# Two loads traced under another engine's squares, two casts moved to GpSimd, and three frame loads moved ahead of the small rows, at the beginning of a streaming encoder trunk

## The chip, the core and the metric

The kernel runs on one core of one Trainium2 chip. The metric is the device time of one execution in microseconds (us). Each run is timed several times; the profile is of one more execution, which has a time of its own and, inside it, a span from its first to its last instruction. The core's engines work side by side, each through its own list of instructions in order: PE (TensorE, matmul and transpose), DVE (VectorE), ACT (ScalarE), POOL (GpSimd) and SP (SyncE, which here issues most of the loads and stores). An instruction can carry waits on semaphores that other engines and transfers raise; until they are met, the engine stands and everything behind it in its list stands too.

## The reference

One layer over 2080 frames (2048 of a prompt, 32 of a running stream) of width 1024, all in float32:

```python
hn = rmsnorm(h, g_mix)
proj = hn @ w_in                       # 1024 x 3072
hA, bA, cA, zA, vB, zB = split(proj)   # six blocks of 512 columns
yA = bA * (causal width-3 conv of cA * hA + bias) * silu(zA)
yB = (windowed mean of vB - vB, mapped per group, scaled) * silu(zB)
h = h + concat([yA, yB]) @ w_out
h = h + (p @ w_ple) * sigmoid(rmsnorm(h, g_ple) @ w_gate)
y = rmsnorm(h, g_final)
```

The histories of the convolution and of the pooling are outputs as well. Only the first two lines concern the change: the norm of the first frames and their first products with `w_in`.

## The kernel before

**Arithmetic.** A float32 product is made of three products of parts: each operand is split into a rounded high part ("hi") and the rest ("lo"), and hi·hi, hi·lo and lo·hi are added up in one PSUM bank. The hi part is a cast (ACT `copy`), the lo part a subtraction (DVE `tensor_tensor`).

**Blocks.** The prompt's frames are worked on in blocks of 416 (three tiles of 128 rows and one of 32). In the first stage two blocks are in memory at once. Frames come in with rows on partitions, are squared and summed on ACT (`sumsq`), POOL makes the reciprocal root of the mean from the sum in two small instructions (`rstd_of`, lines 70 and 74), DVE scales the rows, PE transposes them into PSUM, and from there the hi and lo parts are made.

**Beginning.** For block 0 the order is written out by hand (lines 608 to 683): three tiles and the two 32-row pieces `short0` are loaded, `first_normal` scales, `first_turn` transposes, `first_hi` and `first_lo` make the parts. The raw columns of the first three weights (`zb`, `v`, `c`; 512 KB each) are loaded by `raw_weight`, and their hi parts are cast on ACT (lines 673 and 691), their lo parts subtracted on DVE (lines 682 and 695). `first_products` then runs hi·hi, weight-hi·frame-lo and weight-lo·frame-hi, each for `zb`, `v` and `c` in turn, eight matmuls at a time. Between these products the generator `second_block` is stepped: it loads the three tiles of block 1 (line 712), scales them with `normal` (line 406), transposes them, splits them into hi and lo (line 724: ACT, line 78, then DVE, line 81), copies them back to memory (line 725) and forms sums and differences (from line 734). After that come `zb`, `v` and `c` of block 1 with the usual three parts, matmul by matmul (line 572), and then the rest of the stage.

**Six small vectors** (convolution weights, biases, histories) are loaded into the tile `rows` (lines 751 to 756), turned by one transpose into `pv`, and the pooling weights are loaded into `raw_pw` (line 769).

**What sets the order.** The kernel is traced in program order and a planner then orders each engine's list by costs it assumes; the lists are fixed when the program is built. `keep_in_program_order` (in `in_turn`) ties an instruction to the one traced before it on its engine. `tc.issue_after(ins)` ties what its block traces *on the engine of* `ins` to a place behind `ins` in that engine's list; it is a matter of order in the list, not a wait. Buffers come in rings: `xin` has five tiles for frames, `raws` four for raw columns, `ps_m` six PSUM banks. A load into a ring's next tile waits until the last reader of the tile's former content is done. SP's loads also share eight semaphores in turn, so that the ninth load waits until the first has landed, and so on.

Of the kernel before, what the change touches and what calls it, by code (L numbers as in the profile page):

```python
# [28 lines left out]
KH = KC // 2  # L29
# [5 lines left out]
def trunk(ctx, tc, x_p, x_s, c_conv, c_pool, p_p, p_s, g_mix, w_in, conv_w, conv_b, pool_w,  # L35
          pool_scale, w_out, g_ple, w_gate, w_ple, g_fin, y_p, y_s, sc_p, sp_p, sc_s, sp_s):
    nc = tc.nc
# [29 lines left out]
    def rstd_of(ssq, n, name, r=None):  # L67

        ms = sm.tile([P, 1], F32, tag="ms", name=f"ms_{name}")
        nc.gpsimd.tensor_scalar(ms[:n], ssq[:n], scalar1=1.0 / D, scalar2=EPS,  # L70
                                op0=ALU.mult, op1=ALU.add)
        if r is None:
            r = sm.tile([P, 1], F32, tag="rstd", name=f"rstd_{name}")
        nc.gpsimd.tensor_tensor(r[:n], ms[:n], nhalf[:n], op=ALU.pow)  # L74
        return r
# [10 lines left out]
    g_bc = const.tile([P, D], F32, name="g_bc")  # L86
    junk = const.tile([P, D], mybir.dt.bfloat16, name="junk")

    def sumsq(x, n, name, r=None, later=False):
        ssq = sm.tile([P, 1], F32, tag="ssq", name=f"ssq_{name}")  # L90
        ins = nc.scalar.activation(junk[:n], x[:n], AF.Square, accum_out=ssq[:n])  # L91
        if later:
            tc.keep_in_program_order(ins)
        return rstd_of(ssq, n, name, r)
# [206 lines left out]
    def ring4(t, name):  # L301
        return t.tile([P, D], F32, tag="t", name=name)
# [21 lines left out]
    with ExitStack() as s1:  # L324
# [45 lines left out]
        def fill(n, t):  # L370

            for _ in range(n):
                tc.keep_in_program_order(nc.tensor.transpose(t[:, :P], ident, ident))
# [7 lines left out]
        def x_rows(tb, c):  # L381
            r = tb * NB + c * P
            if c < 3:
                return x_p[r:r + P]
            return x_p[r:r + DEC] if tb < 4 else x_s

        def x_load(name, rows):

            t, at = ring4(xin, f"xt_{name}"), 0
            for src in rows:  # L390
                m = src.shape[0]
                nc.sync.dma_start(t[at:at + m], src)
                at += m
            return t, at, f"x{name}"

        def x_stat(x, later=False):

            t, n, name = x
            return t, n, sumsq(t, n, name, later=later)

        def x_tile(name, rows):
            return x_stat(x_load(name, rows))
# [103 lines left out]
        def raw_weight(kind, j, name, ring=raw_ring):  # L506
            t = ring(f"raw_{name}")
            col = cols[kind] * WA + j * P
            nc.sync.dma_start(t, w_in[:, col:col + P].rearrange("(k p) n -> p k n", p=P))
            return t  # L510
# [101 lines left out]
        def in_turn(ins):  # L612
            tc.keep_in_program_order(ins)
# [34 lines left out]
        def first_tile(c):  # L648
            first_normal(first_x[c])
            turned_x[c] = first_turn(c, first_x[c])  # L650
            if c < 3:
                fill((2, 3, 2)[c], short_bank)


        for c in range(3):
            first_x.append(x_stat(ahead0[c], True))
        first_tile(0)
        first_hi(0, 0)
        first_x.append(x_stat(short0, True))
# [7 lines left out]
        first_hi(2, 0)  # L667
        first_tile(3)
        first_hi(2, 1, nc.vector.tensor_copy)
        raw = raw_weight("zb", 0, "firstzb")  # L670
        first_zb = [wtile(f"w_firstzb_{half}") for half in range(2)]
        for half, t in enumerate(first_zb):
            in_turn(nc.scalar.copy(t[:, :, 0], raw[:, half * KH:half * KH + KH]))
        for half in range(2):
            first_hi(3, half)
        for c in range(4):
# [8 lines left out]
        first_los = {}  # L685

        def other_first(kind):
            raw = raw_weight(kind, 0, f"first{kind}")
            ts = [wtile(f"w_first{kind}_{half}") for half in range(2)]
            for half, t in enumerate(ts):  # L690
                nc.scalar.copy(t[:, :, 0], raw[:, half * KH:half * KH + KH])

            def los():
                for half, t in enumerate(ts):
                    nc.vector.tensor_tensor(t[:, :, 1], raw[:, half * KH:half * KH + KH], t[:, :, 0].bitcast(F32),
                                            op=ALU.subtract)

            first_los[kind] = los
            return ts
# [7 lines left out]
        def second_block():  # L707

            spans = [(c, slice(c * P, min(NB, c * P + P))) for c in range(4)]
            xs = []  # L710
            for c in range(3):
                x = x_tile(f"1_{c}", [x_rows(1, c)])
                normal(x)
                xs.append((x, slice(0, P)))
                yield
            xs.append((short0, slice(DEC, 2 * DEC)))
            whole = []
            for c, cs in spans:
                x, ts = xs[c]

                turned = x[0].rearrange("p (k t) -> p k t", k=KC)[:, :, :ts.stop - ts.start]
                for half, q in enumerate(("12", "22")):
                    pt = turn(x, half, f"pt1_{c}_{half}", bank)[:, :, ts]
                    put(B0[q][:, :, :, cs], pt)
                    nc.scalar.copy(turned[:, half * KH:half * KH + KH], pt)
                whole.append((turned[:, :KH], turned[:, KH:]))
                yield
            op = lambda o, a, b, op=ALU.subtract: nc.vector.tensor_tensor(o, a, b, op=op)
            for c, cs in spans:
                p12, p22 = whole[c]  # L730
                n = cs.stop - cs.start
                t1, t3, t2, t4 = (ftile(f"f{t}_1_{c}")[:, :, :n] for t in range(4))
                part = lambda q, h: B0[q][:, :, h, cs].bitcast(F32)
                op(t1, p12, part("11", 0))
                op(t3, p22, p12)
                op(t1, t1, part("11", 1))
                op(t2, p22, t1)
                put(B0["T2"][:, :, :, cs], t2)
                put(B0["T1"][:, :, :, cs], t1)
                put(B0["T3"][:, :, :, cs], t3)  # L740
                op(t4, part("21", 0), t2)
                op(t4, t4, part("21", 1), ALU.add)
                to_memory(p_d["T4"], f"T4_0_{c}", t4, c * P, n)
                yield
# [463 lines left out]
        for gi, tbs in enumerate(GROUPS):  # L1208
            if gi == 2:

                frames_in.close()
                t = slot("hn_4")
# [37 lines left out]
    with ExitStack() as s2:  # L1250
# [113 lines left out]
        for i in range(0, NT - 1, 2):  # L1364
            with tc.issue_after(loaded[-1].ins):
                x = [load_rows(xh, "x", i + b, x_p) for b in range(2)] if i else [first_x, second_x]
# [12 lines left out]
            if last:  # L1379
                x = load_rows(xh, "x", NT - 1, x_p, x_s)  # L1380
# [20 lines left out]
        def ring(what, i):  # L1401
            if what == "pps":
                return st.tile([P, 2, 2, P], F32R, tag="t", name=f"pps_{i}")
            if what == "out" and i not in rest_e[-LATE:]:
                return cmb.tile([P, D], F32, tag="c", name=f"eout_{i}")
            return ring4(ya, f"e{what}_{i}")
# [8 lines left out]
        for k in range(KH):  # L1415
            raw = [ring4(t, f"wg_r{k}_{i}") for i, t in enumerate(((ya, ya), (ya, xh), (xh, xh), (ya, ya))[k])]
# [249 lines left out]
```

## Time and profile before

| what | value |
|---|---|
| times of three runs, us | 927.29, 930.17, 5190.86 |
| median of them, us | 930.17 |
| time of the profiled execution, us | 929.13 |
| its span, us | 927.2 |
| granted PE clock, mean | 0.998 |
| DVE, ACT, POOL busy, share of the span | 78%, 52%, 17% |

The span lies 1.93 us below the execution's own time. The third run is far off the others and stands outside any reading. On the page, busy times are sums over the span, "idle before" is the time an engine stood before an instruction and what ended it, and the line numbers are those of the code above. In the timeline, merged rows carry a count (x3), their start and the time until the last of them ends. SPq is the list of SP's transfers: its rows say when a transfer was issued, not when it landed.

### The profile page before, as it was taken

The numbers are of one execution on the slowest core, as the hardware profiler recorded it, in microseconds if no ns is written. First come the engines' busy times: TensorE is split into PE (matmuls) and PEld (weight loads), VectorE is DVE, ScalarE is ACT, GpSimd is POOL, SyncE is SP. The second block draws the span as 40 slices with busy tenths as digits, with TensorE's granted clock in tenths as the row PEclk, the third lists the DMA queues.
The fourth block names the chain that finished last, engine by engine and source line by source line (L and its number), as shares of the span: only waits on it lengthen the run. The fifth ranks groups of instructions, "written<-read, shape, count | busy, mean of one in ns | idle before, by whom it ended". The sixth has DMA issues, their size and how long they took to land.

```text
span 927.2 us, 13211 instructions
## 1 busy us (share of the span) xinstructions
PE 912.1 (98%) x4553; PEld 826.3 (89%) x4553; DVE 719.7 (78%) x1221; ACT 483.5 (52%) x895; POOL 159.6 (17%) x299
## 2 busy tenths in 40 slices
PE   8999999999999999999999999999999999999996
PEld 6999998999999999999999987888878768888885
DVE  6996989999577869795777678765558658889885
ACT  7743565654345545443544356334336755565563
POOL 3111222121001234110000010111203301111113
PEclk9999999999999999999999999999999999999999
DMA  8357687798936567769655349866787964676663
GB/s 249 98 147 217 168 259 217 230 298 294 410 114 188 173 167 229 187 227 309 184 166 178 122 178 295 266 188 177 227 240 234 377 220 142 227 252 203 200 197 114
DMA packets 135279, 198.58 MB, mean 214 GB/s; under 512 B 12796, under 2 KB 99740, under 8 KB 133933
## 3 DMA queue, kind: packets, MB, share of 16 engines
q1 hardware_dynamic: 115661, 136.65, 47.5%
q0 software_dynamic: 16816, 55.65, 18.8%
q10 hardware_dynamic: 2736, 5.44, 1.8%
q8 instruction: 36, 0.59, 0.3%
q14 instruction: 30, 0.25, 0.1%
HBM read 133.84 MB, written 63.84 MB: 213 GB/s over the span
## 4 chain that ended last, share of the span: by engine, by line
PE 60%; DVE 2%; DMA 2%; issue 1%; ACT 1%; POOL 0%; POOLq 0%; SPq 0%; DVEq 0%; ACTq 0%
PE x_g L161 8%; PE x_o L161 8%; PE z_g L161 4%; PE z_o L161 4%; PE e L105 3%; PE x_zab L572 3%; PE x_ch L572 2%; PE y_g L161 2%; PE x_zbv L572 2%; PE b L572 2%; PE v L572 2%; PE c L572 2%; PE zb L572 2%; PE h L572 2%; PE za L572 2%; PE y_o L161 2%
## 5 line engine op out<-in xcount | busy, mean ns | idle before, releaser
L78 ACT CAST y_S<-y_fS 128x512 fp32r<-128x512 f32 x32 | 19.5, 622 | 40.4 <-PE x_o L161 19.8
L105 PE MATMUL e<-wq,pps 128*128 128x512 f32 (+1 forms) x156 | 36.2, 391 | 0.9 <-DMA pps<-pp_d 0.9
L161 PE MATMUL x_g<-wg_b,g_S 128*128 128x512 f32 x128 | 36.7, 392 | 0.0
L161 PE MATMUL x_o<-wo_b,y_S 128*128 128x512 f32 x128 | 35.8, 391 | 0.0
L105 PEld LDWEIGHTS e<-wq,pps 128*128 128x128 f32 (+1 forms) x156 | 28.2, 182 | 8.2 <-ACT wg_a L78 1.3
L572 PE MATMUL z_ch<-B,w_ch_S 128*128 128x416 f32 x168 | 34.3, 352 | 0.0
L572 PE MATMUL x_zbv<-B,w_zbv_S 128*128 128x416 f32 x168 | 34.2, 352 | 0.0
L572 PE MATMUL z_zbv<-B,w_zbv_S 128*128 128x416 f32 x168 | 34.2, 352 | 0.0
L572 PE MATMUL z_zab<-B,w_zab_S 128*128 128x416 f32 x168 | 34.2, 352 | 0.0
L572 PE MATMUL x_zab<-B,w_zab_S 128*128 128x416 f32 x168 | 34.1, 351 | 0.0
L572 PE MATMUL x_ch<-B,w_ch_S 128*128 128x416 f32 x168 | 34.0, 351 | 0.0
L572 PEld LDWEIGHTS x_ch<-B,w_ch_S 128*128 128x128 f32 x168 | 31.4, 188 | 0.3
L572 PEld LDWEIGHTS x_zab<-B,w_zab_S 128*128 128x128 f32 x168 | 31.3, 188 | 0.3
L572 PEld LDWEIGHTS x_zbv<-B,w_zbv_S 128*128 128x128 f32 x168 | 31.3, 188 | 0.4
L572 PEld LDWEIGHTS z_zab<-B,w_zab_S 128*128 128x128 f32 x168 | 31.3, 188 | 0.3
L572 PEld LDWEIGHTS z_zbv<-B,w_zbv_S 128*128 128x128 f32 x168 | 31.3, 188 | 0.3
L572 PEld LDWEIGHTS z_ch<-B,w_ch_S 128*128 128x128 f32 x168 | 31.3, 188 | 0.3
L78 ACT CAST y<-y 128x512 fp32r<-128x512 f32 x24 | 14.8, 618 | 30.7 <-PE x_o L161 14.4
L406 DVE SCALAR_TENSOR_TENSOR xt<-xt,rstd_x,g_bc 128x1024 f32<-128x1024 f32 (+2 forms) x14 | 17.9, 1282 | 16.2 <-POOL rstd_x L74 16.2
L70 POOL TENSOR_SCALAR ms_f<-ssq_f 128x1 f32<-128x1 f32 (+1 forms) x15 | 7.6, 509 | 131.0 <-ACT junk L91 131.0
L1269 DVE TENSOR_TENSOR c_o<-x_o,x 128x512 f32<-128x512 f32 x14 | 9.7, 690 | 25.1 <-PE x_o L161 25.1
L161 PEld LDWEIGHTS x_o<-wo_b,y_S 128*128 128x128 f32 x128 | 23.9, 188 | 5.6 <-ACT y_S L78 0.4
(584 smaller groups left out, 2697.1 us busy)
## 6 DMA issues: line engine op xcount, KB each, us to landing
y<-y_d SPq DMA_DIRECT2D x16, 512.0 KB, 10.2
x<-in_x_prompt_dram SPq DMA_DIRECT2D x16, 512.0 KB, 6.0
h_d<-x SPq DMA_DIRECT2D x16, 512.0 KB, 4.3
h<-h_d SPq DMA_DIRECT2D x16, 512.0 KB, 3.9
xt<-in_x_prompt_dram SPq DMA_DIRECT2D x15, 512.0 KB, 7.4
e<-e_d SPq DMA_DIRECT2D x15, 512.0 KB, 4.5
out_dram<-h POOLq DMA_DIRECT2D x14, 512.0 KB, 3.1
p_dT<-T POOLq DMA_DIRECT2D x12, 512.0 KB, 6.2
```

What stands on the lines that cost most here:

```text
L70: nc.gpsimd.tensor_scalar(ms[:n], ssq[:n], scalar1=1.0 / D, scalar2=EPS, op0=ALU.mult, op1=ALU.add)
L78: ins = nc.scalar.copy(hi, src)
L105: nc.tensor.matmul(ps[:n], pps[:, a, k, :n], wp[k][b][:, cs], start=k + q == 0, stop=k == 1 and q == 2)
L161: nc.tensor.matmul(ps[:n], lhs[:, k, a, :n], w[b][:, k], start=start and k + q == 0, stop=k == KH - 1 and q == 2, skip_group_check=True)
L406: nc.vector.scalar_tensor_tensor(xt[:n], xt[:n], r[:n], g_bc[:n], op0=ALU.mult, op1=ALU.mult)
L572: nc.tensor.matmul(ps[:, :NB], lhs[:, k, x], b[:, k, y], start=start and k + q == 0, stop=stop and k == KH - 1 and q == 2, skip_group_chec ...
L1269: add = lambda o, a, b: nc.vector.tensor_tensor(o, a, b, op=ALU.add)
```

## The change

- `sumsq` now notes each square in a list `squares`. The raw columns of `zb` are traced inside `tc.issue_after(squares[0].ins)`, those of `v` and `c` inside `tc.issue_after(squares[1].ins)`, right after the three squares of block 0; they are held in `raw` and `first_raws`. The squares are on ACT, the loads on SP.
- The two hi casts of `zb` are traced on `nc.gpsimd` instead of `nc.scalar`.
- The loads of block 1's three tiles are traced ahead (`ahead1`): the first behind the raw columns, the other two behind the `zb` casts, all of them before the small rows. `second_block` then only squares them.

In the list of SP in the changed program the first eight transfers (`g_mix`, three tiles and two short pieces of frames, `zb`, `v`) and the ninth (`c`) stand as before and with the waits they had before; the three tiles of block 1 follow them, and then the six small rows, the pooling weights and the next raw columns. In ACT's list the two `zb` casts are gone, one of the two `g_bc` copies stands in their place, and the cast of the pooling weights stands behind the three squares of block 1. In DVE's list the three `normal` instructions of block 1 stand in front of the four lo subtractions of `v` and `c` (behind them before), and one subtraction of the differences of block 1 stands earlier than the last splits. In PE's list the `pv` transpose stands twenty-six matmuls later, and two single matmuls (one of `c`, one of `h`) no longer stand in front of block 1's `zb` products. From the work on that stands at about 80 us in the profile of before, all lists are as before.

```diff
@@ -86,9 +86,12 @@
+    squares = []
+
     def sumsq(x, n, name, r=None, later=False):
         ssq = sm.tile([P, 1], F32, tag="ssq", name=f"ssq_{name}")
         ins = nc.scalar.activation(junk[:n], x[:n], AF.Square, accum_out=ssq[:n])
+        squares.append(ins)
         if later:
             tc.keep_in_program_order(ins)
         return rstd_of(ssq, n, name, r)
@@ -654,6 +657,12 @@
         for c in range(3):
             first_x.append(x_stat(ahead0[c], True))
+
+        with tc.issue_after(squares[0].ins):
+            raw = raw_weight("zb", 0, "firstzb")
+        with tc.issue_after(squares[1].ins):
+            first_raws = {kind: raw_weight(kind, 0, f"first{kind}") for kind in ("v", "c")}
+        ahead1 = [x_load("1_0", [x_rows(1, 0)])]
         first_tile(0)
         first_hi(0, 0)
@@ -667,10 +676,11 @@
         first_hi(2, 1, nc.vector.tensor_copy)
-        raw = raw_weight("zb", 0, "firstzb")
         first_zb = [wtile(f"w_firstzb_{half}") for half in range(2)]
         for half, t in enumerate(first_zb):
-            in_turn(nc.scalar.copy(t[:, :, 0], raw[:, half * KH:half * KH + KH]))
+            in_turn(nc.gpsimd.tensor_copy(t[:, :, 0], raw[:, half * KH:half * KH + KH]))
+        ahead1.append(x_load("1_1", [x_rows(1, 1)]))
+        ahead1.append(x_load("1_2", [x_rows(1, 2)]))
         for half in range(2):
             first_hi(3, half)
@@ -685,7 +695,7 @@
         def other_first(kind):
-            raw = raw_weight(kind, 0, f"first{kind}")
+            raw = first_raws[kind]
             ts = [wtile(f"w_first{kind}_{half}") for half in range(2)]
@@ -709,7 +719,7 @@
             for c in range(3):
-                x = x_tile(f"1_{c}", [x_rows(1, c)])
+                x = x_stat(ahead1[c])
                 normal(x)
```

## The prediction

> **What bounds the kernel now.** I read the page's head and then busy time by stretches, to see what a gain or loss at the beginning is worth at the end.
>
> ```profile
> span 927.2 us, 13211 instructions
> ```
>
> ```profile
> 15.00:35.00 20.00, 18.98 (x112) 17.85 (x113) 18.70 (x34) 16.39 (x37) 4.97 (x6) 1.00 0.67 198
> ```
>
> ```profile
> 35.00:135.00 100.00, 100.00 (x539) 98.18 (x539) 89.87 (x167) 51.78 (x101) 18.01 (x23) 1.00 0.61 174
> ```
>
> The columns are length, then busy time of PE, its weight loads, DVE, ACT and POOL, then the clock. From 35 to 135 us PE is never idle: whatever the beginning shifts there is no gap to swallow it, and none to refund it, so the shift goes through to the end. The lists of the engines are the same again by then. The whole effect is therefore the moment at which PE enters that stretch. From 15 to 35 us PE idles 1.02 us, of which 0.63 lies before its first product (15.63, below); 0.39 is all that better order behind that start can win.
>
> The second view is the timeline, engine by engine, up to that first product.
>
> ```profile
> 9.29 1.06 ACT L91 ACTIVATE junk<-xt 128x1024 bf16<-128x1024 f32 x1 [1.93 <-DMA xt<-in_x_prompt_dram]
> ```
>
> ```profile
> 10.80 0.55 POOL L74 TENSOR_TENSOR rstd_x<-ms_x,nhalf 128x1 f32<-128x1 f32 x1
> ```
>
> ```profile
> 11.56 2.73 DVE L620 SCALAR_TENSOR_TENSOR xt<-xt,rstd_x,gm 128x512 f32<-128x512 f32 x4
> 14.21 0.67 DVE L642 CAST B<-pt 128x512 fp32r<-128x512 f32 x1
> 14.81 1.27 DVE L646 TENSOR_TENSOR B<-pt,B 128x512 fp32r<-128x512 f32 x2
> ```
>
> ```profile
> 13.88 0.93 PE L629 MATMUL pt<-ident,xt 64*128 64x64 f32 x8
> 15.63 1.75 PE L600 MATMUL zb<-B,w_firstzb 128*128 128x416 f32 x8 [0.83 <-DVE B L646]
> ```
>
> Read backwards: the first product waits 0.83 us for a DVE subtraction that frees its PSUM bank. It is the first of the two at 14.81 (two take 1.27, one 0.67, so one step is 0.60 and the first ends near 15.5). DVE has run without a gap since 11.56, when the scale of the third tile was ready (POOL, 10.80 + 0.55), and that hung on the third tile's landing: ACT stood 1.93 us for it. So the third tile's transfer sets the start, not ACT's casts.
>
> **The change part by part.**
>
> *The hold-back of the raw columns.* Its square is on ACT, the loads are on SP, and the tie reaches only instructions on the square's own engine.
>
> ```profile
> 3.49 0.48 SPq L509 DMA_DIRECT2D raw_firstzb<-in_w_in_dram  x1
> 4.01 0.87 SPq L509 DMA_DIRECT2D raw_firstv<-in_w_in_dram  x1
> 4.92 5.05 SPq L509 DMA_DIRECT2D raw_firstc<-in_w_in_dram  x1
> ```
>
> In the changed list these three stand in the same places with the same waits. They still share the transfers with the third tile, it still lands near 9.2, and the first product still starts near 15.6. Cost and gain: zero.
>
> *The two casts on POOL.* No row shows this cast on POOL, so the nearest bound it; the third row is POOL's last work before it.
>
> ```profile
> L1535 POOL TENSOR_TENSOR hg<-h,g_bc 128x512 f32<-128x512 f32 x1 | 2.0, 1985 | 0.0
> ```
>
> ```profile
> masks.py:199 POOL TENSOR_SCALAR_AFFINE_SELECT ident<-ident 128x128 f32<-128x128 f32 x1 | 0.3, 283 | 0.0
> ```
>
> ```profile
> 12.31 0.54 POOL L74 TENSOR_TENSOR rstd_x<-ms_x,nhalf 64x1 f32<-64x1 f32 x1
> ```
>
> ```profile
> 13.76 1.15 ACT L673 CAST w_firstzb<-raw_firstzb 128x512 fp32r<-128x512 f32 x2
> 14.84 0.43 ACT L642 CAST B<-pt 128x128 fp32r<-128x128 f32 x2
> ```
>
> POOL is free from 12.31 + 0.54 = 12.85. Two inputs of that size took 1.99 us; one input of a quarter of it took 0.28, so 1.13 for four quarters. I take 1.13, the row with one input; the bounds are 0.28 and 1.99. The raw columns landed by 13.76 at the latest, since ACT started there without a wait. Halves are then ready at 13.98 and 15.11; at worst at 15.75 and 17.73. PE wants the first at 15.6 and the second four matmuls later (1.75 for eight, so 0.87): 16.5. Taken: no wait; at worst 1.2 us, which the DVE limit below would mostly cover again.
>
> ACT loses 1.15 us there, but its next step, the casts at 14.84, waits for the transposes that end at 13.88 + 0.93 = 14.81. Nothing starts earlier. One `g_bc` copy (0.54, half of 1.08) drops into the hole.
>
> *ACT behind it.*
>
> ```profile
> 16.20 1.15 ACT L691 CAST w_firstc<-raw_firstc 128x512 fp32r<-128x512 f32 x2
> 17.24 1.08 ACT L703 COPY g_bc<-gm 128x512 f32<-128x512 f32 x2
> 18.20 0.65 ACT L78 CAST pw<-raw_pw 128x512 fp32r<-128x512 f32 x1
> 19.04 1.06 ACT L91 ACTIVATE junk<-xt 128x1024 bf16<-128x1024 f32 x1 [0.19 <-DMA xt<-in_x_prompt_dram]
> 20.00 0.19 ACT L91 ACTIVATION_READ_ACCUMULATOR junk<-xt 128x1 f32 x1
> 20.32 1.06 ACT L91 ACTIVATE junk<-xt 128x1024 bf16<-128x1024 f32 x1
> ```
>
> ```profile
> 21.80 1.06 ACT L91 ACTIVATE junk<-xt 128x1024 bf16<-128x1024 f32 x1 [0.32 <-DMA xt<-in_x_prompt_dram]
> ```
>
> With one copy moved forward and the `pw` cast moved back, block 1's squares start at 17.24 + 0.54 = 17.78 instead of 19.04, then every 1.28 (19.04 to 20.32). A sum is there 1.15 behind its start (19.04 to 20.00 + 0.19): 18.93, 20.21, 21.49. That needs the tiles. In before ACT stood 0.19 for the first and 0.32 for the third, so they landed near 19.0 and 21.7, 1.4 us a tile. Now they queue straight behind `c`, which had landed by 16.20, as its cast started without a wait: 17.6, 19.0 and 20.4 at the latest. Taken: in time; at worst as before, since their place in the list only moved forward.
>
> *DVE, where the order costs.* The three scales now stand in front of the lo parts of `v` and `c`, and DVE runs in order, so it stands wherever a scale's statistic is late.
>
> ```profile
> 18.20 1.27 DVE L682 TENSOR_TENSOR w_firstzb<-raw_firstzb,w_firstzb 128x512 fp32r<-128x512 f32 x2
> ```
>
> ```profile
> 22.79 2.47 DVE L406 SCALAR_TENSOR_TENSOR xt<-xt,rstd_x,g_bc 128x1024 f32<-128x1024 f32 x2
> 25.70 1.28 DVE L406 SCALAR_TENSOR_TENSOR xt<-xt,rstd_x,g_bc 128x1024 f32<-128x1024 f32 x1 [0.44 <-POOL rstd_x L74]
> ```
>
> ```profile
> 20.27 0.24 POOL L70 TENSOR_SCALAR ms_x<-ssq_x 128x1 f32<-128x1 f32 x1 [7.42 <-ACT junk L91]
> 20.59 0.88 POOL L74 TENSOR_TENSOR rstd_x<-ms_x,nhalf 128x1 f32<-128x1 f32 x1
> ```
>
> ```profile
> 23.36 0.76 POOL L70 TENSOR_SCALAR ms_x<-ssq_x 128x1 f32<-128x1 f32 x1
> 24.20 1.47 POOL L74 TENSOR_TENSOR rstd_x<-ms_x,nhalf 128x1 f32<-128x1 f32 x1
> ```
>
> From sum to statistic POOL took 1.20 (20.27 to 21.47) and, beside the scales, 2.31 (23.36 to 25.67); beside nothing 0.82 would do (0.27 to the root's start and its 0.55). DVE is free at 19.47. First tile: sum 18.93, POOL 19.01, ready 20.21: idle 0.7. The scale step is 1.19 (2.47 less 1.28). For the other two, POOL works beside a scale; I take the middle of 0.82 and 2.31, 1.57: ready at 21.86 (DVE free 21.4, idle 0.4) and 23.43 (DVE free 23.1, idle 0.3). Together 1.4; bounds 0.5 (0.82 each) and 3.1 (2.31 each, one behind the other).
>
> ```profile
> 28.55 0.69 DVE L81 TENSOR_TENSOR B<-pt,B 128x512 fp32r<-128x512 f32 x1 [0.37 <-ACT B L78]
> ```
>
> ```profile
> 31.41 0.69 DVE L81 TENSOR_TENSOR B<-pt,B 128x512 fp32r<-128x512 f32 x1 [0.37 <-ACT B L78]
> ```
>
> ```profile
> 33.69 0.48 DVE L81 TENSOR_TENSOR B<-pt,B 128x128 fp32r<-128x128 f32 x2
> ```
>
> ```profile
> 33.97 0.34 PE L572 MATMUL c<-B,w_firstc 128*128 128x416 f32 x1
> 34.15 0.45 PE L572 MATMUL h<-B,w_h 128*128 128x416 f32 x1
> 34.44 4.50 PE L572 MATMUL zb<-B,w_firstzb 128*128 128x416 f32 x23
> ```
>
> The meeting point is the second `zb` matmul of block 1: it needs the last frame split of DVE, at 33.69. Before, DVE idled 0.44 + 0.37 + 0.37 = 1.18 on the way. After, one subtraction more stands ahead (0.60), and I keep one of the waits for ACT: 33.69 + 0.60 − 1.18 + 1.4 + 0.37 = 34.9, split done 0.24 later, PE on at about 35.2. Before, PE went on at 34.44, but with the single matmuls of `c` and `h` done (0.47, from 33.97): like for like 33.97. **Sum: +1.2 us.** With the low bound (0.5, no ACT wait) the split is done by 33.4 and PE is held by its own work: between −0.4 and 0. With the high one (3.1 and 0.74) 36.95 + 0.24 gives +3.3.
>
> *What is moved past on SP.* The three tiles stand ahead of six small rows, `raw_pw` and the next raw columns. The rows feed `pv`, which stands 26 matmuls later, 5.7 us by 1.75 for eight; that, and for the pooling cast its place behind the squares, is their cover.
>
> ```profile
> 19.54 0.38 SPq L509 DMA_DIRECT2D raw_h<-in_w_in_dram  x1
> ```
>
> ```profile
> 26.50 0.63 ACT L78 CAST w_h<-raw_h 128x512 fp32r<-128x512 f32 x1
> ```
>
> `raw_h` now also waits for the third tile's landing, 19.6 to 21.7: nothing, or up to 2.2 us, and its cast at 26.50 stands in ACT's list in front of copies that free PSUM. The next raw columns (`za`) take the tile of `v` and wait for its lo part, near 26 (the third scale, 23.43 + 1.28, and two steps of 0.60); their cast follows the `zb` product that ends at 38.94 (34.44 + 4.50), which covers a transfer as long as `raw_h` had at most (7.0).
>
> **The rivals.**
>
> *The statistics are in time* (for it: squares 1.26 earlier; against: POOL at 0.76 and 1.47 beside the scales). DVE idles 0.5, PE wins up to its 0.39: 928.8.
>
> *POOL is held out while a scale runs.* For it: 23.36 + 0.76 ends just behind the first scale's end, 24.20 + 1.47 behind the second's. Then each tile waits for the one before: 3.1 idle, 932.4. The Trainium skill ("SBUF — State Buffer", Who interferes with whom) says that a DVE instruction with two SBUF inputs and a GpSimd instruction that reads SBUF exclude each other whole. The two rows agree with that; 20.59, with 0.88 beside single subtractions, shows a shorter hold.
>
> *The tiles land as late as before.* For it: `c`'s issue took SP 5.05, so SP's queue was full there; against: they stand seven transfers further forward. The third square then starts at 21.80, its sum is there at 22.95 and the scale ready at 24.6 by the same 1.57 and POOL's 0.08 in front, 1.2 later than taken: 931.5.
>
> *The hold-back does act* (against: the list). The third tile would land earlier by up to the 1.93 that ACT stood for it. How much of that DVE can use is not seen; I take two thirds, a start near 14.3: 929.13 − 1.3 = 927.8.
>
> *The POOL cast is far dearer.* Slower by over 2% (18.6 us; about what a measurement of this kernel can tell from no change) if the second half is ready at 35.1: 12.85 + 2d, d = 11.1 us, against 1.99 for the dearest row of that size; 948 and more.
>
> **How the numbers follow.** Profiled execution 929.13, span 927.2 and 1.93 around it; forecast 929.13 + 1.2 = 930.3, which is also near the median of 930.17 (the two usable runs are 927.29 and 930.17). Chances: forecast 0.46, statistics in time 0.25, POOL held out 0.13, late tiles 0.10, hold-back 0.04, dear cast 0.02. The forecast and the next three reach from 928.8 to 932.4; runs of one kernel differ by up to 1.8 from the profiled one, so 927.3 to 932.9. Within 2%: 0.97; faster 0.01; slower 0.02, the dear cast.
>
> **What would show it.** Right: SP's nine first transfers as before, ACT still standing for the third tile, first product near 15.6; squares of block 1 near 17.8; DVE idle in front of the three scales, released by POOL; the second `zb` matmul of block 1 waiting for DVE near 35. Wrong: a first product before 15, a wait of PE for POOL's casts, no idle in front of the scales, or any new wait of PE behind 40 us.

## The result, and the profile after

The changed kernel took 929.88 us (median of 22 runs, 928.30 to 932.85), the kernel before 928.63 us (median of 22 runs beside them). The ratio is 1.0017, 95% interval 1.0010 to 1.0023: slower by 1.6 us, less than a tenth of the 2% at which a verdict would change, but not zero. The forecast was 930.3, +1.2 on the profiled execution.

Three places of the timeline of the changed kernel carry the reading. First PE, from the first product to block 1's `zb` products (start, length, engine, line, what; in brackets the idle time in front and what ended it):

```profile
14.28 1.73 PE L603 MATMUL zb<-B,w_firstzb 128*128 128x416 f32 x8 [0.83 <-DVE B L649]
...
25.85 0.60 PE L416 MATMUL pt<-ident,xt 128*128 128x128 f32 x4
28.00 0.66 PE L416 MATMUL pt<-ident,xt 128*128 128x128 f32 x4 [1.56 <-ACT xt L735]
...
33.37 0.46 PE L575 MATMUL zb<-B,w_firstzb 128*128 128x416 f32 x1 [0.17 <-ACT B L78]
```

Second DVE around block 1's scales, and POOL's small instructions that these wait for, in the same kernel:

```profile
6.92 2.77 DVE L623 SCALAR_TENSOR_TENSOR xt<-xt,rstd_x,gm 128x512 f32<-128x512 f32 x4 [4.74 <-POOL rstd_x L74]
...
16.85 1.28 DVE L692 TENSOR_TENSOR w_firstzb<-raw_firstzb,w_firstzb 128x512 fp32r<-128x512 f32 x2
18.85 1.28 DVE L409 SCALAR_TENSOR_TENSOR xt<-xt,rstd_x,g_bc 128x1024 f32<-128x1024 f32 x1 [0.72 <-POOL rstd_x L74]
20.85 1.28 DVE L409 SCALAR_TENSOR_TENSOR xt<-xt,rstd_x,g_bc 128x1024 f32<-128x1024 f32 x1 [0.72 <-POOL rstd_x L74]
22.85 1.28 DVE L409 SCALAR_TENSOR_TENSOR xt<-xt,rstd_x,g_bc 128x1024 f32<-128x1024 f32 x1 [0.72 <-POOL rstd_x L74]
```

```profile
9.17 0.19 POOL L70 TENSOR_SCALAR ms_x<-ssq_x 128x1 f32<-128x1 f32 x1 [0.92 <-ACT junk L93]
...
11.47 1.17 POOL L681 CAST w_firstzb<-raw_firstzb 128x512 fp32r<-128x512 f32 x2
17.62 0.56 POOL L70 TENSOR_SCALAR ms_x<-ssq_x 128x1 f32<-128x1 f32 x1 [4.99 <-ACT junk L93]
18.26 0.55 POOL L74 TENSOR_TENSOR rstd_x<-ms_x,nhalf 128x1 f32<-128x1 f32 x1
18.90 1.28 POOL L70 TENSOR_SCALAR ms_x<-ssq_x 128x1 f32<-128x1 f32 x1
20.27 0.55 POOL L74 TENSOR_TENSOR rstd_x<-ms_x,nhalf 128x1 f32<-128x1 f32 x1
```

Third ACT, at the third square of block 0, at the first square of block 1 and at the copy that PE waits for:

```profile
7.94 1.06 ACT L93 ACTIVATE junk<-xt 128x1024 bf16<-128x1024 f32 x1 [0.60 <-DMA xt<-in_x_prompt_dram]
...
16.37 1.07 ACT L93 ACTIVATE junk<-xt 128x1024 bf16<-128x1024 f32 x1
...
27.36 0.59 ACT L735 COPY xt<-pt 128x512 f32<-128x512 f32 x1 [1.69 <-DVE B L81]
```

POOL's 128 x 1 instruction at 18.90 takes 0.19 us for block 0 (`ms_x`, first row), although a scale runs on DVE there too (the four end at 9.69); that scale reads its gains `gm` from PSUM, block 1's reads them from the copy `g_bc` in SBUF. Here it lasts 1.28 and ends at 20.18, 0.05 behind the scale that began at 18.85. Only then comes the root, 0.55, and only then the next scale. So DVE stands 0.72 us three times, 2.16 in all, where it stood 0.44 before. Counted from the first product, the splits of block 1's first tile start 1.09 us later (26.64 in the changed kernel, 26.90 before): 1.72 more of idle time, less one subtraction of `c` (0.60) that now stands behind them. ACT's copy at 27.36 stands behind the first of these splits, and PE's transposes at 28.00 stand behind the copy: 1.56 us, where the same transposes waited 0.17 before, for another instruction of ACT. That they write the bank which the copy frees is inferred from what released them.

The stretch behind it is as it was:

```profile
15.00:35.00 20.00, 18.23 (x110) 16.98 (x109) 17.84 (x33) 14.69 (x31) 4.78 (x6) 1.00 0.57 171
35.00:135.00 100.00, 100.00 (x540) 98.17 (x539) 88.89 (x166) 51.49 (x102) 18.06 (x23) 1.00 0.59 173
```

PE busy 100.00 of 100 us again (second column). So the beginning can be measured by one distance: from the start of the first product to the start of the `za` products, between which PE has the same matmuls in both kernels. The `za` rows of before and after:

```profile
57.48 0.73 PE L572 MATMUL za<-B,w_za 128*128 128x416 f32 x3
```

```profile
57.58 0.72 PE L575 MATMUL za<-B,w_za 128*128 128x416 f32 x3
```

Before: 57.48 − 15.63 = 41.85. After: 57.58 − 14.28 = 43.30. That is +1.45 us, against +1.6 measured by the times (+0.9 to +2.1).

The two profiled executions do not show it in their spans: 926.9 after, 927.2 before. The changed one's first product happened to start 1.35 earlier (14.28 for 15.63), and far behind, a wait for a transfer (`pps`) was 0.33 for 0.86. −1.35 + 1.45 − 0.53 = −0.4, and −0.3 was seen. Whether the earlier start belongs to the change is the first question below.

### The profile page after: what moved, and what is told of

The parts are those of the page before. It is cut to its first block, busy times and chain, and to the rows that moved or that the text cites. A ratio compares the mean times of both kernels' runs of the same rounds, so it can differ in the third digit from the quotient of the medians.

```text
span 926.9 us, 13213 instructions
## 1 busy us (share of the span) xinstructions
PE 910.9 (98%) x4553; PEld 825.5 (89%) x4553; DVE 719.5 (78%) x1221; ACT 482.8 (52%) x893; POOL 161.0 (17%) x301
## 4 chain that ended last, share of the span: by engine, by line
PE 61%; DVE 2%; issue 1%; DMA 1%; ACT 1%; POOL 1%; POOLq 0%; DVEq 0%; ACTq 0%
PE x_g L164 9%; PE x_o L164 8%; PE z_g L164 4%; PE z_o L164 4%; PE e L108 3%; PE x_zab L575 3%; PE x_ch L575 2%; PE y_g L164 2%; PE x_zbv L575 2%; PE za L575 2%; PE c L575 2%; PE v L575 2%; PE zb L575 2%; PE h L575 2%; PE b L575 2%; PE y_o L164 2%
```

## The experiments

For every run the same three numbers were read: when the third square starts (the third tile has then landed), when the first product starts, and the distance to `za`. Times are ratios to the kernel before on the same chip, from 11 or 12 runs each (22 for the first row of the change).

| run | third square | first product | to `za` | ratio, 95% interval |
|---|---|---|---|---|
| before | 9.29 | 15.63 | 41.85 | 1 |
| before, again | 8.42 | 14.76 | 41.85 | 0.9998 (0.9988 to 1.0009) |
| the change | 7.94 | 14.28 | 43.30 | 1.0017 (1.0010 to 1.0023) |
| the change, again | 8.42 | 14.76 | 43.28 | 1.0026 (1.0016 to 1.0035) |
| change, casts on ACT | 8.36 | 14.75 | 43.28 | 1.0021 (1.0011 to 1.0031) |
| change, tiles back | 8.61 | 14.96 | 42.70 | 1.0024 (1.0015 to 1.0032) |
| before, POOL's casts alone | 8.21 | 14.55 | 42.71 | 1.0019 (1.0009 to 1.0029) |
| the same, splits first | 8.02 | 14.53 | 42.23 | 1.0014 (1.0005 to 1.0023) |
| change, lo parts first | 9.28 | 15.63 | 43.10 | 1.0008 (0.9998 to 1.0018) |
| the same, loads held back | 8.53 | 14.87 | 43.10 | 1.0005 (0.9992 to 1.0018) |
| change, gains from PSUM | 9.27 | 15.61 | 42.13 | 1.0005 (0.9997 to 1.0014) |
| the same, splits first | 9.25 | 15.60 | 41.72 | 1.0007 (0.9993 to 1.0021) |

The distance repeats to 0.02 us in two executions of one kernel; the times leave about ±1 us open. Behind `za` the distance lasts: at 135 us, PE's products of all profiles but the two with the splits first stand within 0.03 us of the kernel before, counted from `za`. So the distance says what the beginning costs. It and the times do not always agree: against "lo parts first", "tiles back" has the shorter distance (42.70, 43.10) and the longer time (1.0024, 1.0008). From `za` to the end of the span these two profiles took 871.6 and 869.5 us, but the two of the kernel before took 869.7 and 872.4 (1.6 of the difference is a fall of the clock, last section), so one profile each cannot say whether something behind `za` belongs to the kernels.

### Both kernels once more

Nothing is edited.

> The kernel before once more, nothing edited: a second sample of when the third tile lands and of how far two sets of times of one program lie apart. Theory A (the landing varies from execution to execution with one list on SP: third squares started between 7.94 and 9.28 in four profiles with the list of the changed kernel and at 9.29 in the profile before): a third square anywhere from 7.9 to 9.3, the first product 6.34 behind it, 41.8 to 41.9 us from the first product to za, ratio 0.9995 to 1.0005. Theory B (the changed kernel's list brings the third tile earlier): third square at 9.2 to 9.4 again.

> The changed kernel once more, nothing edited. Theory A (landing by chance, the rest fixed): third square anywhere from 7.9 to 9.3, first product 6.34 behind it, 43.2 to 43.4 us from the first product to za, ratio to the kernel before 1.001 to 1.0022. Theory B (early landing belongs to the change): third square at 7.9 to 8.1 again.

Measured: the third square at 8.42 in both, the first product 6.34 later in both, and the distances 41.85 and 43.28. The early start belongs to neither kernel. The list of SP is the same up to that tile in all the profiles of the table but one (the run with the loads held back), and in two more below; in these 13 the third square started at 9.25 to 9.29 four times and at 7.94 to 8.61 nine times. What follows the landing is nearly fixed: the first product starts 6.34 to 6.51 us behind the third square. The loss is there in both pairs, 1.45 and 1.43 us. The ratio of the changed kernel, 1.0026, lies above the 1.0022 expected, with an interval that reaches down to it.

### The lo parts back in front of the scales

```diff
                 if b:
                     next(second)
                     next(second)
+                    first_los["v"]()
+                    first_los["c"]()
...
                         if kind == "zb":
                             next(second)
-                            first_los["v"]()
-                        elif kind == "v":
-                            first_los["c"]()
```

> The changed kernel with one thing put back as it was: the lo parts of the second and third first weights (v and c) stand on DVE ahead of block 1's three scales. Theory A (the scales stand on DVE waiting for POOL's second small operation of each tile, which POOL cannot finish while a scale runs; 2.16 us of DVE idle in the changed kernel; behind it the last split of block 0 comes late, ACT's copy and with it the PSUM bank of block 1's second tile come late, and PE stands 1.56 us at line 416): the idle in front of the scales falls below 0.5 us, the PE wait of 1.56 at line 416 goes, and the time falls 1.2 to 1.9 us against the changed kernel, a ratio to the kernel before of 0.9995 to 1.0005. Theory B (the other edits, POOL's casts or the order of the transfers, cost the time): ratio 1.0015 to 1.002 as in the changed kernel, the wait at line 416 stays.

Measured: 43.10, a gain of 0.20 where 1.2 to 1.9 was expected. PE's wait at line 416 did go, but a new one of 0.86 stands at block 1's first `zb` matmul, and DVE still stands 0.73, 0.71 and 0.53 in front of the scales. DVE and POOL in this run:

```profile
18.19 1.27 DVE L691 TENSOR_TENSOR w_firstzb<-raw_firstzb,w_firstzb 128x512 fp32r<-128x512 f32 x2
19.39 1.27 DVE L704 TENSOR_TENSOR w_firstv<-raw_firstv,w_firstv 128x512 fp32r<-128x512 f32 x2
20.60 1.28 DVE L704 TENSOR_TENSOR w_firstc<-raw_firstc,w_firstc 128x512 fp32r<-128x512 f32 x2
22.60 1.29 DVE L409 SCALAR_TENSOR_TENSOR xt<-xt,rstd_x,g_bc 128x1024 f32<-128x1024 f32 x1 [0.73 <-POOL rstd_x L74]
```

```profile
18.96 2.97 POOL L70 TENSOR_SCALAR ms_x<-ssq_x 128x1 f32<-128x1 f32 x1 [4.98 <-ACT junk L93]
22.01 0.55 POOL L74 TENSOR_TENSOR rstd_x<-ms_x,nhalf 128x1 f32<-128x1 f32 x1
```

POOL's first instruction began at 18.96 and ended at 21.93, 0.05 behind the last of DVE's subtractions (20.60 + 1.28). The 2.4 us of work that were meant to cover POOL's arithmetic kept POOL out instead. The theory was half right: the scales do stand for POOL, but not for want of work in front of them. The ratio, 1.0008, is also above the 1.0005 expected, with an interval that takes it in.

### The loads really held back

On top of the last edit, ACT writes one element of each raw tile behind the squares, so that SP's loads have to wait for ACT.

```diff
-        def raw_weight(kind, j, name, ring=raw_ring):
+        def raw_weight(kind, j, name, ring=raw_ring, behind=None):
...
+            if behind is not None:
+                in_turn(nc.scalar.copy(t[:1, 0, :1], behind[0][:1, :1]))
...
-        with tc.issue_after(squares[0].ins):
-            raw = raw_weight("zb", 0, "firstzb")
+        first_x.append(x_stat(ahead0[0], True))
+        raw = raw_weight("zb", 0, "firstzb", behind=ahead0[0])
```

> The changed kernel with v's and c's lo parts ahead of the scales as in the first run of this call, and with the hold-back made real: ACT writes one element of each raw weight's tile behind the first square (zb) or the second (v, c), so SP's loads of the raw weights wait for ACT. That element costs ACT some 0.2 us three times. Theory A (the first product's start sets the end, and the third tile's landing sets the first product's start): the third square on ACT starts before 8.0 us from the span's start with no raw weight on the queues before it, the first product starts by 14.3, and the ratio to the kernel before is 0.9985 to 0.9995 (0.5 to 1.4 us gained). Theory B (the raw weights' loads do not delay the third tile; the landing varies from execution to execution by itself, 9.29 before and 7.94 after with the same list on SP): ratio 0.9995 to 1.0005, as the first run of this call, and the third tile lands in the same spread. Theory C (held back, the first weight lands too late): POOL's casts wait for it, the first product starts after 15.6, ratio 1.0005 or more.

Measured: the raw weights were issued at 6.33, 7.66 and 8.16 us instead of 3.5 to 5.2, and the third square started at 8.53, inside the spread without the hold-back, as Theory B said. The distance is the 43.10 of the run above, the ratio 1.0005 beside 1.0008. Held-back loads brought no earlier start in this profile; one profile cannot say whether they would keep away the late landings near 9.27.

### POOL's casts: taken out, and alone

```diff
         for half, t in enumerate(first_zb):
-            in_turn(nc.gpsimd.tensor_copy(t[:, :, 0], raw[:, half * KH:half * KH + KH]))
+            in_turn(nc.scalar.copy(t[:, :, 0], raw[:, half * KH:half * KH + KH]))
```

> The changed kernel with the casts of the first weight's hi parts back on ACT instead of POOL. Theory A (DVE's order costs the time, the casts' engine nothing): ratio to the kernel before 1.0010 to 1.0022, the wait at line 416 stays at 1 us or more. Theory B (POOL's casts cost it, by delaying POOL's statistics of block 1 or by the port): the DVE idle in front of the scales falls below 1 us and the ratio is 0.9995 to 1.0005.

Measured: 43.28 and 1.0021, PE's wait at line 416 at 1.46, DVE's three waits of 0.72 as in the changed kernel: without POOL's casts the loss stays whole. (One of the four lo parts stands in front of the scales in this run.) The converse, the same line changed in the kernel before and nothing else:

> The kernel before with one edit alone: POOL instead of ACT casts the hi parts of the first weight; raw loads and tiles stay where they were. This moves DVE's list further down: three of the subtractions of block 1's first tile (line 725 of this file) stand ahead of the splits of the third tile, where two stood. Theory A (the opening is bound by DVE from the first lo part of block 0 to the last split of block 1, so every operation or wait that comes into that stretch delays PE's entry by its length; the list costs about 0.7 us): from the first product's start to the start of the za products 42.5 to 42.9 us where the kernel before has 41.85, ratio to the kernel before 1.0005 to 1.0012. Theory B (POOL's casts themselves hold DVE or PE up): PE or DVE waits for POOL's cast, at line 600 or 682. Theory C (the casts cost nothing): 41.8 to 42.0 us, ratio 0.9995 to 1.0003.

Measured: 42.71, so +0.86; the time, 1.0019, lies above what was expected, with an interval that reaches down to it. No engine waits for POOL's cast. The lists differ further down, as said there (the subtractions are line 728); DVE, PE and ACT of this run:

```profile
29.03 0.68 DVE L728 TENSOR_TENSOR f<-xt,B 128x512 f32<-128x512 f32 x1
29.63 0.69 DVE L728 TENSOR_TENSOR f<-xt 128x512 f32<-128x512 f32 x1
30.23 0.69 DVE L728 TENSOR_TENSOR f<-f,B 128x512 f32<-128x512 f32 x1
30.83 1.28 DVE L81 TENSOR_TENSOR B<-pt,B 128x512 fp32r<-128x512 f32 x2
```

```profile
33.37 0.45 PE L572 MATMUL zb<-B,w_firstzb 128*128 128x416 f32 x1 [1.20 <-ACT B L78]
```

```profile
31.04 0.72 ACT L78 CAST B<-f 128x512 fp32r<-128x512 f32 x1
...
31.97 1.18 ACT L725 COPY xt<-pt 128x512 f32<-128x512 f32 x2
32.92 0.56 ACT L78 CAST B<-pt 128x128 fp32r<-128x128 f32 x2
```

and PE and ACT of the kernel before:

```profile
33.48 0.46 PE L572 MATMUL zb<-B,w_firstzb 128*128 128x416 f32 x1 [0.22 <-ACT B L78]
```

```profile
33.06 0.54 ACT L78 CAST B<-pt 128x128 fp32r<-128x128 f32 x2
33.46 0.63 ACT L725 COPY xt<-pt 128x512 f32<-128x512 f32 x1
33.94 0.66 ACT L78 CAST B<-f 128x512 fp32r<-128x512 f32 x1
```

Three subtractions of the next step stand ahead of the third tile's splits, but PE does not wait for DVE: it stands 1.20 us (0.22 before) at block 1's first `zb` matmul, for ACT's hi part of the last tile (`B<-pt`, 128x128). In both runs ACT has no idle time from `zs` (26.39 here, 27.50 before) to these casts. Here two entries stand in front of them that stood behind: the cast of a subtraction's result (`B<-f`), which follows the subtractions, and one copy back (`xt<-pt`), some 0.5 us each. Counted from the first product, the last hi parts start 0.94 us later than before (32.92 − 14.55 against 33.06 − 15.63), and PE's wait is 0.98 longer. So Theory A's number came out, but the binding engine was ACT.

### The tiles back at their old place

```diff
-        ahead1 = [x_load("1_0", [x_rows(1, 0)])]
...
-                x = x_stat(ahead1[c])
+                x = x_tile(f"1_{c}", [x_rows(1, c)])
```

> The changed kernel with block 1's three tile loads back at their old place, behind the small rows, which also puts DVE's order back (lo parts of v and c ahead of the scales). Theory A (DVE's order, by the early tiles): no idle in front of the scales, no PE wait at line 416, ratio to the kernel before 0.9995 to 1.0005, within 0.0005 of the run that moves the lo parts alone. Theory B (POOL's casts or the raw loads cost it): ratio 1.0015 or more. Theory C (the earlier tiles are a gain that DVE's order eats up): this run lies over the run that moves the lo parts alone by 0.0005 or more.

Measured: 42.70, and 1.0024. None of the three theories said this: no idle time in front of the scales beyond the 0.44 of before, and still +0.85. It is the run before once more: with the tiles back, the lists are those of POOL's casts alone, since tracing the raw loads earlier moves no entry in any list. So the two edits that do something, the casts and the early tiles, cost 0.86 and 1.43 each by itself and 1.45 together: each makes parts of block 1 late in its own way, and they do not add up. The time of this run, 1.4 to 3.0 us over the kernel before, lies above the 0.85 of the distance; what adds the rest is not shown.

### The gains read from PSUM

```diff
-                normal(x)
+                for half in range(2):
+                    h = x[0][:, half * NH:half * NH + NH]
+                    nc.vector.scalar_tensor_tensor(h, h, x[2], pg[half], op0=ALU.mult, op1=ALU.mult)
```

> The changed kernel with block 1's scales reading the gains from their PSUM tiles, six operations of 512 columns instead of three of 1024 with the copy in SBUF; nothing else is edited. Each scale then has one SBUF input. Theory A (POOL's small operations are held out while DVE runs an operation with two SBUF inputs): POOL's operations of block 1 take 0.19 and 0.55 us each, where they took 1.28 and 0.55, DVE's idle in front of the scales falls from 2.16 us to below 0.8 in all, and from the first product to za 41.4 to 42.2 us instead of 43.30; ratio to the kernel before 0.999 to 1.0003. Theory B (the idle is only the length of POOL's two steps behind ACT's squares, 0.82 us for each tile, whatever DVE runs): the idle stays at 1.8 us or more and the ratio at 1.001 or more.

Measured: 42.13. DVE and POOL of this run:

```profile
20.17 4.04 DVE L725 SCALAR_TENSOR_TENSOR xt<-xt,rstd_x,gm 128x512 f32<-128x512 f32 x6 [0.72 <-POOL rstd_x L74]
```

```profile
20.22 0.19 POOL L70 TENSOR_SCALAR ms_x<-ssq_x 128x1 f32<-128x1 f32 x1
20.50 0.55 POOL L74 TENSOR_TENSOR rstd_x<-ms_x,nhalf 128x1 f32<-128x1 f32 x1
21.31 0.19 POOL L70 TENSOR_SCALAR ms_x<-ssq_x 128x1 f32<-128x1 f32 x1 [0.27 <-ACT junk L93]
```

The six scales run without a gap, and beside them POOL's instructions take 0.19 and 0.55. The idle time in front of the scales is 0.72 instead of 2.16, and that wait stands behind two-input subtractions (line 692). One input of each scale moved from SBUF to PSUM, and each scale became two of half the length. The length is not the reason: POOL's 0.19 at 20.22 lie whole inside the first scale, which began at 20.17 (the six take 4.04). This shows the cause: POOL is held out by DVE's instructions with two SBUF inputs. The Trainium skill ("SBUF — State Buffer", Who interferes with whom) states that rule, and that a DVE instruction with at most one SBUF input, outside the modes in which it takes two ports, does not get in GpSimd's way; 1.28 and 0.19 agree with both halves. The ratio, 1.0005, is above the 1.0003 expected, with an interval that takes it in.

What is late next: PE stands 0.70 us at block 1's first `zb` matmul, for ACT's hi part, as with POOL's casts alone, and here too a cast of a subtraction's result stands in front of it.

### The splits fixed ahead of the subtractions

In both runs DVE's eight splits of block 1 are tied in front of the subtractions of the next step. First on POOL's casts alone:

```diff
-                    put(B0[q][:, :, :, cs], pt)
+                    hi, lo = B0[q][:, :, :, cs][:, :, 0], B0[q][:, :, :, cs][:, :, 1]
+                    nc.scalar.copy(hi, pt)
+                    in_turn(nc.vector.tensor_tensor(lo, pt, hi.bitcast(F32), op=ALU.subtract))
...
-                op(t1, p12, part("11", 0))
-                op(t3, p22, p12)
+                in_turn(op(t1, p12, part("11", 0)))
+                in_turn(op(t3, p22, p12))
```

> POOL's casts alone on the kernel before, as in the run of that edit, with DVE's list fixed by hand: all eight splits of block 1's tiles ahead of the subtractions of line 728. Theory A (DVE binds the opening, and the casts cost 0.86 us only because they move three subtractions ahead of the last splits): from the first product to za 41.4 to 41.9 us instead of 42.71, PE's wait of 1.2 us at the second zb product falls below 0.3, ratio to the kernel before 0.9993 to 1.0005. Theory B (the casts cost it in another way): the distance stays at 42.5 us or more. A later cost is open: the subtractions, pushed behind, may make B's T pieces late for x_zbv, which would show as a PE wait near 80 us.

Measured: 42.23, between what the two theories said, so 0.48 of the 0.86 are the subtractions' place. With them `B<-f` went behind the last hi parts on ACT. The copy stayed in front: the last hi parts start 17.95 us behind the first product (17.43 before), and PE still stands 0.70 at the `zb` matmul (0.22 before). The rest is therefore that copy's place in ACT's list. DVE itself stood 0.67 for ACT's hi parts in front of a split. The open point of the expectation came true, in another place: the waits of PE between 56 and 180 us of this run (engine and line, what it waited for, us, times, longest) have one that the kernel before has not, and another of 0.8 (`z_ch` for ACT) follows later:

```profile
PE x_ch L572 <- ACT c_s L970: 1.0, 1, 1.0
```

At 135 us PE is 1.25 later, counted from `za`, than in the kernel before. The ratio of 1.0014 has these in it. Then the same on the gains from PSUM:

> The changed kernel with the gains read from PSUM and the splits of block 1 ahead of the subtractions: both causes of the loss out, everything that the change meant kept. Theory A (those two are all): from the first product to za 41.4 to 41.9 us where the changed kernel has 43.30 and the kernel before 41.85; PE works without a wait over 0.3 us from the first product to za; ratio to the kernel before 0.999 to 1.0003, and not faster by more, since PE's own work is 41.4 us there. Theory B (something else of the change costs time as well): 42.3 us or more, or a ratio over 1.001.

Measured: 41.72, 0.13 under the kernel before, and no wait of PE over 0.18 from the first product to `za`; the beginning is mended, and the two causes are all of the loss up to `za`. In the time it is no gain (1.0007, 0.9993 to 1.0021, where 1.0003 at most was expected). The tie has a price here too: at 135 us PE stands 0.53 later, counted from `za`, than in the kernel before, where the profiles without it agree to 0.03; `x_ch` waits 0.3 of it for ACT, as it waited 1.0 above. That is one profile. No version found beats the kernel before.

### Why POOL was held through a whole row of instructions

In the kernel before, POOL's small instructions of block 1 got in among DVE's subtractions and took 0.24 to 0.88 us each. With the lo parts first, the first one went past four boundaries between two DVE instructions. Two runs, one profile each: with the first weight's casts on ACT, and with DVE copies of one column between the lo parts.

```diff
                                             op=ALU.subtract)
+                    nc.vector.tensor_copy(gap, t[:, 0, 1, :1])
```

> The lo parts of v and c ahead of the scales, as in the first of these runs, and the first weight's casts on ACT. The question is why POOL's first operation was held through four instruction boundaries of DVE there (2.97 us), while in the kernel before it gets in at the next one. Theory A (POOL's cast, or the waits on POOL that DVE's zb parts then carry, have to do with it): POOL's first operation of block 1 takes under 1 us. Theory B (an unbroken row of DVE operations with two SBUF inputs keeps POOL out to its end): 1.5 to 3 us, until DVE stands idle.

> The lo parts of v and c ahead of the scales, and between them DVE copies of one column (128 x 1, one SBUF input), after the second part of v and after each part of c. Theory A (DVE keeps POOL out over an unbroken row of operations with two SBUF inputs, and an operation with one lets it in): POOL's first operation of block 1 ends within 0.3 us behind the first of these copies, some 2.4 us behind the start of DVE's zb parts, and not with DVE's idle time behind the row. Theory B (only idle DVE lets it in): it ends behind the last part of c, as before, 2.9 us long.

Measured: 2.48 us without POOL's casts (past three boundaries), 3.09 with the copies between. POOL of the first run:

```profile
18.32 2.48 POOL L70 TENSOR_SCALAR ms_x<-ssq_x 128x1 f32<-128x1 f32 x1 [6.60 <-ACT junk L93]
```

POOL and DVE of the second:

```profile
17.96 3.09 POOL L70 TENSOR_SCALAR ms_x<-ssq_x 128x1 f32<-128x1 f32 x1 [4.98 <-ACT junk L93]
```

```profile
19.60 0.14 DVE L707 COPY gap<-w_firstv 128x1 f32<-128x1 f32 x1
...
20.33 0.68 DVE L705 TENSOR_TENSOR w_firstc<-raw_firstc,w_firstc 128x512 fp32r<-128x512 f32 x1
20.93 0.14 DVE L707 COPY gap<-w_firstc 128x1 f32<-128x1 f32 x1
```

The first copy ran at 19.60, and POOL's instruction ended only at 21.05, 0.04 behind the last subtraction (20.33 + 0.68) and just before the copy behind it ended. So POOL's cast is not the reason, and copies in the row do not help. (The Trainium skill, in the section named above, counts copies among the instructions that can take the shared ports for themselves; if these did, they were no gap. No run here shows it.) One regularity holds in all fourteen profiles: a first instruction of POOL that is held at block 1 (over 0.19) ends 0.05 to 0.06 us behind the end of a DVE instruction with two SBUF inputs, and a held root (over 0.55) ends 0.41 behind one. Why that is the next DVE instruction to end in one kernel and the last of the row in the other stays open. The one thing seen in common: where it got in, DVE had stood for the `pv` transpose (0.1 to 0.3 us) just before, in five profiles; that was not tried by itself.

The first of these two runs gave a distance of 44.75, which is not to be read as a cost: its PE clock fell (last section). The second gave 43.39.

## Why the prediction came out right, point by point

- **One number, the entry into the stretch without gaps.** Right. PE is busy 100.00 of 100 us behind 35 us, and the distance to `za` (+1.45) says for the change what the times say (+1.6).
- **The hold-back does nothing.** Right: the third tile's landing has the same spread with both kernels. But "a first product before 15" was named as a sign against it, and it appeared at once, at 14.28, just where the rival of an acting hold-back had put it (14.3). The kernel before shows 14.76 when it is run again. The sign was badly chosen: it took one execution's landing for a property of the list.
- **POOL's casts, 1.13 each, no wait.** Mis-sized without effect: 0.58 each (1.17 for two), and no wait. Their indirect cost, the shift of the subtractions, was in the sum as "one subtraction more" on DVE (0.60); alone it comes to 0.86, by way of ACT's list.
- **ACT's squares 1.26 earlier.** Right: 17.78 was forecast with the first product at 15.63, 2.15 behind it; measured 16.37 − 14.28 = 2.09.
- **DVE's idle time in front of the scales, 1.4.** The term that was mis-sized: 2.16. The middle between POOL alone and POOL beside scales was taken for the second and third tile. (Its own steps are 0.74, 0.46 and 0.38, together 1.58; each was rounded down.) The rows show the rule of the rival that was given 0.13: POOL's first instruction is held for the whole scale. That rival's 3.1 was too much, since the root then runs in DVE's idle time at its own 0.55. The row that was read as a shorter hold, 20.59 with 0.88, fits the same rule. This is the subtraction that ran on DVE beside it in the kernel before:

```profile
20.38 0.68 DVE L81 TENSOR_TENSOR pw<-raw_pw,pw 128x512 fp32r<-128x512 f32 x1
```

It ends at 21.06 and the root 0.41 behind it, as the root at 24.20 ends 0.41 behind the second scale (22.79 + 2.47). The hold was shorter because the DVE instruction was.

- **The meeting point, the second `zb` matmul.** Wrong place. In the changed kernel PE met the late splits some 5 us earlier, at the transposes at 28.00, by way of ACT's copy and its PSUM bank; block 1's first `zb` matmul then waited only 0.17. What the transposes of the second tile wait for was not followed.
- **SP's moves at nothing.** Right: no wait of PE between the first product and `za` has a transfer for its releaser.
- **The sum, +1.2.** +1.45 by the distance, +1.6 by the times. The idle time was 0.76 more than taken, and the 0.37 kept for a wait for ACT did not occur: DVE runs from the third scale to past 35 us without a gap. These two errors pull against each other, and the place was wrong, so that the number lies so near is partly luck. At the low bound the split is done by 33.85 (33.69 + 0.60 − 1.18 + 0.5 + 0.24), not 33.4; that is still ahead of 33.97 and changes nothing.

## What to carry to other kernels

When small instructions on POOL feed DVE, ask what DVE runs beside them: instructions with two SBUF inputs lengthened a 0.19 us step to 1.28, and to 2.97 in a row, and work put in front as cover only made that hold longer, while one operand read from PSUM took it away. An edit that only moves work to an idle engine also moves the planner's lists of the others, so compare the lists to the point where they agree again, and look, on every engine that has no idle time there, at what has slipped in front of the last producer of the stage. And measure an effect of 1 us by a distance inside the trace between two events that both kernels share, in more than one execution, since the start and far waits move by as much from one execution to the next.

## What the runs showed of the hardware that was not expected

The landing of block 0's third tile moved by 1.35 us between executions with one and the same list of transfers. A wait far behind, for a transfer of `pps`, was 0.33 and 0.52 in two executions of the changed kernel, 0.86 and 1.87 in two of the kernel before.

In two of fourteen profiles the granted PE clock fell for about 3.4 us in the middle of full work, some 1.1 us behind the end of a wait of PE (1.20 us long at 33.33, 1.87 at 726.54). Waits of 1.20 and 1.82 in other runs brought no fall, so what sets it off is open. The run with the lo parts first and the casts on ACT has it from 35 to 38 us (the last three columns are the clock, the DMA share and GB/s):

```profile
35.00:38.00 3.00, 3.00 (x11) 2.88 (x10) 2.90 (x5) 1.12 (x4) 0.00 (x0) 0.53 0.00 0
```

The clock is 0.53, and 23 `zb` matmuls took 6.06 us there instead of the 4.50 of the kernel before. In the second profile of the kernel before it hit the `e` matmuls behind 726 us (18.19 us for 72, 16.61 in the first). One such event costs as much as the change that was studied.
